# The sample group's states two at a time, in a hybrid decoder step on one core

## The chip, the cores and the metric

The kernel runs on one core of a Trainium2 chip. The metric is the device time of one execution in microseconds; of three runs of the kernel before the median is given. A core has TensorE (PE; matrix products and transposes), VectorE (DVE), ScalarE (ACT), GpSimd (POOL), and SyncE (SP), whose queue issues the DMAs here. Each works through its own instruction stream in order.

## The reference

One layer of a decoder serves a prompt (1024 tokens behind 16 learned ones) and a sample group of 8 sequences with one new token each. Two kinds of heads stand side by side: 8 delta-net heads, with a state S of 128 x 128 per head and sequence, and 4 matrix heads (mLSTM), with a state C of 128 x 256. For the sample group a step is, per sequence and head, with one token (L = 1), cut from the chunked form:

```python
u = _rms_norm(x, norm_w) @ w_in               # q, k, v, gates for both kinds of heads
# delta-net head, one token: kS = k @ S, qS = q @ S
v_new = beta * (v - exp(g) * kS)
o     = exp(g) * qS + (q . k) * v_new
S_new = exp(g) * S + outer(k, v_new)
# matrix head, one token
num   = dec * (q @ C) + ws * (q . k) * v
C_new = dec * C + outer(ws * k, v)
y = concat(gated, normed heads) @ w_out ; x + y, then a last RMSNorm
```

All states go out again as outputs; each is read and written once. The states are 8 x 8 x 128 x 128 and 8 x 4 x 128 x 256 numbers of 4 bytes, 4 MB each.

## The kernel before

The projection by `w_in` is computed in float32 as three products of high and low parts (tiles `pjg`, `pjm`, `pjz`, `pjo`, `pjzm`: 128 x 128 weights against some 350 tokens). This stream of products is the filler: `filler` (L1891) yields four products at a time, and all else is written as generators ("threads") that a planner, `Plan` (L65 to L247), steps through while it records the program. The planner has a clock for each engine, reckons each instruction's time by its size (`note`, L99), and steps a thread when the planned time of what it yielded has come; if none is due, TensorE gets filler. So one fixed order per engine is written down. A thread that yields a tile is due when the tile is done by the plan, plus 2.5 us where a DMA made it (`DMA`, L72, and `when`, L178), or plus the thread's own margin, for the samples 1.5 us, and 1.0 more behind GpSimd (L179 to L180). A DMA is planned as 0.45 us of generation, 0.65 of delay, its bytes over 360 KB per us (220 for rows that are spread over all partitions), and 0.9 at the end for a load or 0.45 for a store (L108 to L113), behind the DMAs planned before it.

The sample group's states are worked on by one thread, `samples` (L1963): `gdn_sample` (L1130) for the delta-net heads, then `mlstm_sample` (L1377). A state of one head, or half a matrix head, is a tile of 128 x (8 x 128): eight sequences side by side, 512 KB. Two buffers, `db` and `ebuf[0]`, take turns (`sb`), and `ebuf[1]` (`vb`) holds the new values. For one state in turn, before the change:

- TensorE multiplies, for each of the 8 sequences, 32 columns (`knf` or `qf`) with that sequence's 128 columns of the state, in column tiles of 32: four products side by side fill 128 rows of one bank (L1190 to L1192, L1423 to L1425). In the trace float32 products have two passes each, so the 8 are 16.
- ScalarE copies the results, TensorE turns them (two transposes), and VectorE takes the wanted columns and makes the new values, 128 x 8.
- TensorE turns the new values to 8 x 128, ScalarE copies them, they go to DRAM (`vb_d`), and come back spread over all 128 partitions (`vb`).
- GpSimd multiplies `vb` by the key, VectorE multiplies the state by its decay (L1224, L1441), then adds `vb` (L1226, L1443), and the state is stored.

The next state is loaded into the other buffer in the meantime. For the matrix heads the new values are the projected ones, so `vb_d` is filled at the head's start.

Meanwhile the prompt's chains run: `mlstm_chain` (L1273) steps through nine chunks a head (tiles `mup`, `mnm`, `C`, `mpm`), and later `gate` (L1482) scales and turns the heads' outputs (`ht`, `hT`), with scales in `rsg` that `head_norms` (L1583) computes. When the samples are done, `places` (L1643) gives their buffers to the output weights.

Of the kernel before, what the change touches and what calls it, by code (L numbers as in the profile page):

```python
# [12 lines left out]
F32 = mybir.dt.float32  # L13
# [7 lines left out]
P = 128  # L21
# [4 lines left out]
NS = 8  # L26
# [270 lines left out]
def hymba_kernel(ctx: ExitStack, tc: tile.TileContext, a: dict, o: dict):  # L297
# [17 lines left out]
    def room(tag):  # L315
        return plan.room(tag, BANKS[tag])
# [133 lines left out]
    rsg = gp.tile([P, GH + MH, 8], F32, name="rsg")  # L450
# [32 lines left out]
    nrow = wk.tile([1, D], F32, tag="tmp", name="nrow", bufs=1)  # L483
# [645 lines left out]

    def gdn_sample():  # L1130
# [47 lines left out]
        rows = [e.rearrange("p a b -> p (a b)")[:, 384:512] for e in (wa, wb)]  # L1178
# [3 lines left out]
        sp.dma_start(sb[0], a["s_S"][0])  # L1182
        for h in range(GH):
            s_ = sb[h % 2]
            yield s_
            yield kn
            h0 = min(h, GH - 2)
            yield room("k")
            at = pst2(f"sA{h}")
            for b in range(NS):  # L1190
                g, j = divmod(b, 4)
                pe.matmul(at[32 * j : 32 * j + 32, P * g : P * g + P], knf[:, 16 * h0 : 16 * h0 + 32], s_[:, b, :], start=True, stop=True)  # L1192
            yield at
            for g in range(2):
                act.copy(rows[g], at[:, P * g : P * g + P])
            yield rows[1]
            for g in range(2):
                pe.transpose(at[:, 256 + P * g : 256 + P * g + P], rows[g], ident)
            yield at

            def of(i):
                c = 256 + 16 * (h - h0) + 8 * i
                return at[:, c : c + 33 * NS - 32 : 33]

            dve.tensor_tensor(out=sn[:, 3, h], in0=of(0), in1=eg[:, h], op=ALU.mult)
            dve.scalar_tensor_tensor(out=sn[:, 3, h], in0=vv[:, h], scalar=0.5, in1=sn[:, 3, h], op0=ALU.mult, op1=ALU.subtract)
            dve.tensor_tensor(out=sn[:, 3, h], in0=sn[:, 3, h], in1=bet[:, h], op=ALU.mult)
            dve.tensor_tensor(out=sn[:, 4, h], in0=of(1), in1=eg[:, h], op=ALU.mult)
            dve.tensor_tensor(out=sn[:, 5, h], in0=sn[:, 3, h], in1=r[:, 5, h], op=ALU.mult)
            dve.tensor_tensor(out=sn[:, 4, h], in0=sn[:, 4, h], in1=sn[:, 5, h], op=ALU.add)  # L1210
# [4 lines left out]
            vsb = wk.tile([NS, P], F32, tag="vsb", name=f"vsb{h}")  # L1215
            act.copy(vsb, vp[0:NS, 0:P])
            sp.dma_start(vb_d[8 * h : 8 * h + 8], vsb)
# [159 lines left out]
    def mlstm_sample():  # L1377
# [27 lines left out]
        rows = wa.rearrange("p a b -> p (a b)")[:, 256:512]  # L1405
# [3 lines left out]
        sp.dma_start(sb[0], a["s_C"][0, 0])  # L1409
        for h in range(MH):  # L1410
            for i in range(2):
                yield room("k")
                vp = pst2(f"mvt{h}_{i}")
                pe.transpose(vp[0:NS, 0:P], msam[:, 2 + i, h], ident)
                vsb = wk.tile([NS, P], F32, tag="vsb", name=f"mvsb{h}_{i}")
                act.copy(vsb, vp[0:NS, 0:P])
                sp.dma_start(vb_d[h, i], vsb)
            for i in range(2):
                s_ = sb[i]
                yield s_  # L1420
                yield room("k")
                qt = pst2(f"mqc{h}_{i}")
                for b in range(NS):  # L1423
                    g, j = divmod(b, 4)
                    pe.matmul(qt[32 * j : 32 * j + 32, P * g : P * g + P], qf, s_[:, b, :], start=True, stop=True)  # L1425
                vb = ebuf[1]
                sp.dma_start(vb, vb_d[h, i].partition_broadcast(P))
                if (h, i) != (MH - 1, 1):
                    sp.dma_start(sb[1 - i], a["s_C"][h + i, 1 - i])
                yield qt  # L1430
                act.copy(rows, qt[:, 0:256])
                yield rows
                for g in range(2):
                    pe.transpose(qt[:, 256 + P * g : 256 + P * g + P], rows[:, P * g : P * g + P], ident)
                qc = qt[:, 256 + 8 * h : 256 + 8 * h + 33 * NS - 32 : 33]
# [46 lines left out]
    def gate(kt_, wcol):  # L1482
# [15 lines left out]
        for c in range(8):  # L1498
            act.activation(ht[:, c], ht[:, c], AF.Copy, scale=rsg[:, hh, c : c + 1])
# [556 lines left out]
```

## Time and profile before

| | |
|---|---|
| runs, us | 1205.81, 1203.74, 1205.92; median 1205.81 |
| profiled execution, us | 1202.72 |
| its span, first to last instruction, us | 1200.9 |
| TensorE products busy | 1184.0 us, 99% |
| VectorE busy | 852.2 us, 71% |
| ScalarE busy | 602.4 us, 50% |
| GpSimd busy | 487.9 us, 41% |
| first and last product of the delta-net states, us | 643.6, 809.4 |
| first and last product of the matrix states, us | 867.4, 968.2 |

Busy times of engines overlap. TensorE's products are pipelined, and an entry's length is that of one pass from its start to its modelled end; what a product costs the stream is read from one start to the next. An idle time stands in brackets behind the instruction that it precedes, with what ended it.

### The profile page before, as it was taken

The numbers are of one execution on the slowest core, as the hardware profiler recorded it, in microseconds if no ns is written. First come the engines' busy times: TensorE is split into PE (matmuls) and PEld (weight loads), VectorE is DVE, ScalarE is ACT, GpSimd is POOL, SyncE is SP. The second block draws the span as 40 slices with busy tenths as digits, with TensorE's granted clock in tenths as the row PEclk, the third lists the DMA queues.
The fourth block names the chain that finished last, engine by engine and source line by source line (L and its number), as shares of the span: only waits on it lengthen the run. The fifth ranks groups of instructions, "written<-read, shape, count | busy, mean of one in ns | idle before, by whom it ended". The sixth has DMA issues, their size and how long they took to land.

```text
span 1200.9 us, 23024 instructions
## 1 busy us (share of the span) xinstructions
PE 1184.0 (99%) x8314; PEld 1105.9 (92%) x8314; DVE 852.2 (71%) x2069; ACT 602.4 (50%) x1894; POOL 487.9 (41%) x648
## 2 busy tenths in 40 slices
PE   9999999999999999999999999999999999999997
PEld 7999999999999999999999999999999999876885
DVE  6789787587968588864356665546767665887986
ACT  7544455667565666554544453336543433333544
POOL 3105977827685756864012404230011111441432
PEclk9999999999999999999999999999999999999999
DMA  6032212212221221122122443535778878574352
GB/s 242 19 97 86 81 47 83 87 43 72 69 75 43 89 73 55 36 75 61 43 84 70 154 126 119 174 123 172 273 273 286 305 269 297 204 270 132 107 159 87
DMA packets 87084, 154.86 MB, mean 129 GB/s; under 512 B 26793, under 2 KB 48513, under 8 KB 86970
## 3 DMA queue, kind: packets, MB, share of 16 engines
q1 hardware_dynamic: 86776, 153.23, 38.1%
q8 instruction: 65, 1.06, 0.4%
q14 instruction: 49, 0.40, 0.1%
q10 hardware_dynamic: 194, 0.17, 0.0%
HBM read 107.65 MB, written 45.71 MB: 128 GB/s over the span
## 4 chain that ended last, share of the span: by engine, by line
PE 82%; DVE 9%; issue 5%; ACT 1%; POOL 1%; DMA 1%; POOLq 0%; SPq 0%; DVEq 0%; ACTq 0%
PE pjg L56 20%; PE pjm L56 13%; PE pjo L56 7%; PE pjz L56 7%; PE op L56 7%; PE pjzm L56 7%; PE up L56 4%; PE tp L56 3%; PE sk L56 2%; PE mnm L56 2%; DVE left L56 1%; PE mup L56 1%; PE hT L56 1%; DVE owl L56 1%; PE kk L56 1%
## 5 line engine op out<-in xcount | busy, mean ns | idle before, releaser
L56 PE MATMUL pjg<-xht,whg 128*128 128x350 f32 (+6 forms) x624 | 197.6, 324 | 1.0 <-ACT xht L56 1.0
L56 PE MATMUL pjg<-xlt,whg 128*128 128x350 f32 (+6 forms) x624 | 197.1, 323 | 0.0
L56 PE MATMUL pjg<-xht,wlg 128*128 128x350 f32 (+6 forms) x592 | 191.1, 326 | 0.0
L56 POOL TENSOR_TENSOR tmp<-B,E 33x31 f32<-33x31 f32 (+15 forms) x248 | 147.0, 593 | 75.3 <-DMA B<-nd 56.5
L56 POOL TENSOR_TENSOR E<-E,tmp 33x31 f32<-33x31 f32 (+15 forms) x248 | 156.0, 629 | 19.4
L56 PE MATMUL op<-owh,left 128*128 128x512 f32 x448 | 142.0, 396 | 2.1 <-DVE xr L56 1.8
L56 PE MATMUL pjm<-xht,wlm 128*128 128x350 f32 (+2 forms) x384 | 126.4, 329 | 0.0
L56 PE MATMUL pjm<-xht,whm 128*128 128x350 f32 (+2 forms) x384 | 126.4, 329 | 0.0
L56 PE MATMUL pjm<-xlt,whm 128*128 128x350 f32 (+2 forms) x384 | 126.2, 329 | 0.0
L56 PEld LDWEIGHTS pjg<-xht,whg 128*128 128x128 f32 x624 | 116.5, 189 | 1.8 <-issue 1.2
L56 PEld LDWEIGHTS pjg<-xlt,whg 128*128 128x128 f32 x624 | 116.5, 189 | 0.5
L56 PEld LDWEIGHTS pjg<-xht,wlg 128*128 128x128 f32 x592 | 111.0, 189 | 0.4
L56 PEld LDWEIGHTS op<-owh,left 128*128 128x128 f32 x448 | 84.0, 188 | 24.7 <-DVE xr L56 2.6
L56 DVE SCALAR_TENSOR_TENSOR kq<-cr,prm,kq 128x346 f32<-128x346 f32 (+7 forms) x147 | 92.1, 630 | 11.6 <-ACT cr L56 8.3
L56 PE MATMUL op<-owl,left 128*128 128x512 f32 x224 | 88.3, 394 | 0.0
L56 PEld LDWEIGHTS pjm<-xht,wlm 128*128 128x128 f32 x384 | 72.5, 189 | 0.8 <-issue 0.4
L56 PEld LDWEIGHTS pjm<-xlt,whm 128*128 128x128 f32 x384 | 72.4, 188 | 0.6 <-issue 0.4
L56 PEld LDWEIGHTS pjm<-xht,whm 128*128 128x128 f32 x384 | 72.4, 189 | 0.2
L56 POOL TENSOR_TENSOR ebuf<-ebuf,wb 128x1024 f32<-128x1024 f32 x8 | 15.7, 1965 | 122.7 <-DMA ebuf<-mvb_d 122.7
L56 PE MATMUL pjo<-xht,who 128*128 128x344 f32 x192 | 62.3, 324 | 0.6 <-DVE mg L56 0.6
L56 PE MATMUL pjz<-xlt,whz 128*128 128x344 f32 x192 | 62.8, 327 | 0.0
L56 PE MATMUL pjz<-xht,wlz 128*128 128x344 f32 x192 | 62.4, 325 | 0.0
(353 smaller groups left out, 3180.7 us busy)
## 6 DMA issues: line engine op xcount, KB each, us to landing
wrg<-in_wt SPq DMA_DIRECT2D x23, 512.0 KB
left<-c_d SPq DMA_DIRECT2D x40, 256.0 KB
wrm<-in_wt SPq DMA_DIRECT2D x16, 512.0 KB
ht<-h_d SPq DMA_DIRECT2D x16, 512.0 KB
gm<-rows_d SPq DMA_DIRECT2D x8, 576.0 KB
xt<-in_x_p SPq DMA_DIRECT2D x8, 512.0 KB
wrz<-in_wt SPq DMA_DIRECT2D x8, 512.0 KB
h_d<-oo SPq DMA_DIRECT2D x64, 64.0 KB
```

The costliest lines, as they stand in the source:

```text
L56: r = f(*args, **kw)
```

## The change

The states are taken in pairs. Both buffers are loaded, and one group of 16 products in column tiles covers both (one bank of 512 columns). Four columns' worth of rows are copied to a new tile `srow` and turned by four transposes into a second bank. In the delta-net heads the new values of two heads are turned by one transpose (16 x 128) and stored by one DMA; each head's are then spread in turn into the one `vb`. GpSimd no longer multiplies `vb`: it multiplies the state by its decay. VectorE does the rest in eight instructions a state, one a sequence, each `vb` times the key's column plus the decayed state. The next pair is loaded when both states have been read for their stores by the plan.

Beside this, the scales `rsg` become one tile for the delta-net heads and one for each matrix head, `gate` yields that tile, and the first row `nrow` lives under another tag.

```diff
-    rsg = gp.tile([P, GH + MH, 8], F32, name="rsg")
+    rsg = [(gp.tile([P, 1, 8], F32, name=f"rsm{h}"), 0) for h in range(MH)]
+    rsg += [(gp.tile([P, GH, 8], F32, name="rsg"), h) for h in range(1)]
+    rsg += [(rsg[MH][0], h) for h in range(1, GH)]
...
-    nrow = wk.tile([1, D], F32, tag="tmp", name="nrow", bufs=1)
+    nrow = wk.tile([1, D], F32, tag="E", name="nrow", bufs=1)
...
+    srow = gp.tile([P, 4 * P], F32, name="srow")
...
-        sp.dma_start(sb[0], a["s_S"][0])
-        for h in range(GH):
-            s_ = sb[h % 2]
-            yield s_
-            yield kn
-            h0 = min(h, GH - 2)
+        for i in range(2):
+            sp.dma_start(sb[i], a["s_S"][i])
+        for h in range(0, GH, 2):
+            for x in (*sb, kn):
+                yield x
             yield room("k")
             at = pst2(f"sA{h}")
-            for b in range(NS):
-                g, j = divmod(b, 4)
-                pe.matmul(at[32 * j : 32 * j + 32, P * g : P * g + P], knf[:, 16 * h0 : 16 * h0 + 32], s_[:, b, :], start=True, stop=True)
+            for i in range(2):
+                for b in range(NS):
+                    g, j = divmod(b, 4)
+                    g = P * (g + 2 * i)
+                    pe.matmul(at[32 * j : 32 * j + 32, g : g + P], knf[:, 16 * h : 16 * h + 32], sb[i][:, b, :], start=True, stop=True)
             yield at
...
+            turned = pst2(f"sT{h}")
+            for g in range(4):
+                pe.transpose(turned[:, P * g : P * g + P], srow[:, P * g : P * g + P], ident)
...
-            pe.transpose(vp[0:NS, 0:P], sn[:, 3, h], ident)
+            pe.transpose(vp[0 : 2 * NS, 0:P], sn[:, 3, h : h + 2].rearrange("p h b -> p (h b)"), ident)
...
-            sp.dma_start(vb, vb_d[8 * h : 8 * h + 8].partition_broadcast(P))
-            if h + 1 < GH:
-                sp.dma_start(sb[(h + 1) % 2], a["s_S"][h + 1])
-            yield vb
-            pool.tensor_tensor(out=vb, in0=vb, in1=kn[:, h, 0].unsqueeze(2).to_broadcast([P, NS, P]), op=ALU.mult)
-            dve.tensor_tensor(out=s_, in0=s_, in1=eg[:, h].unsqueeze(2).to_broadcast([P, NS, P]), op=ALU.mult)
-            yield vb
-            dve.tensor_tensor(out=s_, in0=s_, in1=vb, op=ALU.add)
-            sp.dma_start(o["s_S"][h], s_)
+            for i in range(2):
+                hi, s_ = h + i, sb[i]
+                sp.dma_start(vb, vb_d[8 * hi : 8 * hi + 8].partition_broadcast(P))
+                pool.tensor_tensor(out=s_, in0=s_, in1=eg[:, hi].unsqueeze(2).to_broadcast([P, NS, P]), op=ALU.mult)
+                yield s_
+                yield vb
+                for b in range(NS):
+                    dve.scalar_tensor_tensor(out=s_[:, b], in0=vb[:, b], scalar=kn[:, hi, 0, b : b + 1], in1=s_[:, b], op0=ALU.mult, op1=ALU.add)
+                yield s_, 0.3
+                sp.dma_start(o["s_S"][hi], s_)
+            if h + 2 < GH:
+                yield plan.read[sb[0].tensor.name]
+                sp.dma_start(sb[0], a["s_S"][h + 2])
+            if h + 2 < GH:
+                yield plan.read[sb[1].tensor.name]
+                sp.dma_start(sb[1], a["s_S"][h + 3])
...
         yield has("rs", hh)
+        yield rsg[hh][0]
```

`mlstm_sample` is changed in the same way (two halves of a head are its pair; its new values are still turned one by one).

TensorE at the first delta-net pair (`sA`: the states' products; `pjm`: projection; `mup`, `mnm`: the prompt chain). Before, the first state's group and then, 112 rows later, the second one's:

```order
L56 MATMUL pjm1_2_2_8853<-xlt_77,whm1_2_8663 128x348
L56 MATMUL pjm1_2_2_8853<-xht_76,wlm1_2_8664 128x348
L56 MATMUL sA0_8881<-db_103,skn_8821 32x128 x8
L56 MATMUL mup0_1_8845<-va1_153,mkt0_1_8847 128x257
L56 MATMUL mnm0_1_8891<-C0_0_8839,mwq0_8607 128x257
```

```order
L56 MATMUL pjm1_3_2_9156<-xht_76,whm1_3_8779 128x348
L56 MATMUL pjm1_3_2_9156<-xlt_77,whm1_3_8779 128x348
L56 MATMUL sA1_9193<-ebuf0_101,skn_8821 32x128 x8
L56 MATMUL pjm1_3_2_9156<-xht_76,wlm1_3_8780 128x348
L56 MATMUL pjm1_3_2_9156<-xht_76,whm1_3_8779 128x348
```

After:

```order
L56 MATMUL pjm1_2_2_8859<-xlt_77,whm1_2_8668 128x348
L56 MATMUL pjm1_2_2_8859<-xht_76,wlm1_2_8669 128x348
L56 MATMUL sA0_8887<-db_103,skn_8826 32x128 x8
L56 MATMUL sA0_8887<-ebuf0_101,skn_8826 32x128 x8
L56 MATMUL mup0_1_8851<-va1_158,mkt0_1_8853 128x257
L56 MATMUL mnm0_1_8905<-C0_0_8845,mwq0_8612 128x257
```

The second group moved up to the first, with nothing between.

SyncE's queue from the first state's store to the loads of the next ones (`wrm`: weights; `mgm`: rows of the prompt's gates; `out_p_C`, `out_p_n`: the prompt's states). Before, with the second load of `db` behind its store by three DMAs:

```order
L56 DMA out_s_S<-db_103 128x1024
L56 DMA wrm2_2_9206<-in_wt 128x1024
L56 DMA vb_d_8826<-vsb1_9279 8x128
L56 DMA ebuf1_102<-vb_d_8826 128x1024
L56 DMA db_103<-in_s_S 128x1024
L56 DMA wrm2_3_9336<-in_wt 128x1024
L56 DMA out_s_S<-ebuf0_101 128x1024
```

After, from the store of the pair's first state; both loads of the next pair stand behind the second store:

```order
L56 DMA out_s_S<-db_103 128x1024
L56 DMA ebuf1_102<-vb_d_8831 128x1024
L56 DMA wrm2_2_9218<-in_wt 128x1024
L56 DMA out_p_C<-C0_8_9195 128x256
L56 DMA out_p_n<-C0_8_9195 128x1
L56 DMA mgm1_9226<-rows_d_84 128x1152
L56 DMA out_s_S<-ebuf0_101 128x1024
L56 DMA db_103<-in_s_S 128x1024
L56 DMA wrm2_3_9340<-in_wt 128x1024
L56 DMA ebuf0_101<-in_s_S 128x1024
```

The load of `db` moved from the middle of the next state's work to the end of the pair's, and that of `ebuf0` from behind `ebuf1`'s spread rows to just behind its own store.

VectorE at the first state's update (`mst`, `hst`: the prompt's norms; `mpm`, `C0`: the prompt chain; `wlm`: a weight's low part). Before:

```order
L56 SCALAR_TENSOR_TENSOR hst_106<-mst0_6_9107 128x1
L56 TENSOR_TENSOR mpm0_8_9140<-mup0_8_9135,mgm0_8606 128x128
L56 TENSOR_TENSOR db_103<-db_103,sgb_97 128x1024
L56 TENSOR_TENSOR wlm2_0_9077<-wrm2_0_8727,whm2_0_9076 128x256
L56 SCALAR_TENSOR_TENSOR C0_8_9166<-C0_7_9125,dec_94,mup0_8_9135 128x257
```

After:

```order
L56 SCALAR_TENSOR_TENSOR hst_106<-mst0_6_9130 128x1
L56 TENSOR_TENSOR mpm0_8_9163<-mup0_8_9158,mgm0_8611 128x128
L56 SCALAR_TENSOR_TENSOR db_103<-ebuf1_102,skn_8826,db_103 128x128 x8
L56 TENSOR_TENSOR wlm2_0_9100<-wrm2_0_8732,whm2_0_9099 128x256
L56 SCALAR_TENSOR_TENSOR C0_8_9195<-C0_7_9148,dec_94,mup0_8_9158 128x257
```

The decay's product has left VectorE, and the eight scaled additions, which read the spread rows in `ebuf1`, stand in its place ahead of the chain's `C0_8`; the addition of before stood 11 rows further down.

## Rows read from the trace of the kernel before

**Rows 1.** the page's part 1: busy us, share of the span, instructions.

```profile
PE 1184.0 (99%) x8314; PEld 1105.9 (92%) x8314; DVE 852.2 (71%) x2069; ACT 602.4 (50%) x1894; POOL 487.9 (41%) x648
```

**Rows 2.** a stretch: us, busy us by engine, granted clock, DMA share, GB/s.

```profile
640.00:985.00 345.00, 342.03 (x2354) 324.44 (x2354) 218.23 (x560) 154.72 (x480) 67.23 (x49) 1.00 0.58 200
```

**Rows 3.** timeline, TensorE: start us, us, instruction, count, [idle before <-releaser].

```profile
668.27 0.32 PE L56 MATMUL pjm<-xht,whm 128*128 128x348 f32 x1
668.43 0.32 PE L56 MATMUL pjm<-xlt,whm 128*128 128x348 f32 x1
668.68 0.64 PE L56 MATMUL sA<-ebuf,skn 128*32 128x128 f32 x16
669.26 0.42 PE L56 MATMUL pjm<-xht,wlm 128*128 128x348 f32 x1
669.52 0.32 PE L56 MATMUL pjm<-xht,whm 128*128 128x348 f32 x1
```

**Rows 4.** timeline, TensorE, one head's two transposes.

```profile
671.93 0.27 PE L56 MATMUL sA<-ident,wa 128*128 128x128 f32 x1
672.04 0.27 PE L56 MATMUL sA<-ident,wb 128*128 128x128 f32 x1
```

**Rows 5.** tile sA: ns min/median/max, first and last start, forms.

```profile
L56 PE MATMUL sA<-db,skn x64: 272/273/298, 643.6 to 788.8; 128*32 128x128 f32 x64
```

**Rows 6.** timeline, TensorE, one head's new values turned.

```profile
676.39 0.32 PE L56 MATMUL pjm<-xht,whm 128*128 128x344 f32 x1
676.55 0.27 PE L56 MATMUL svt<-ident,wa 128*8 128x128 f32 x1
...
676.82 0.32 PE L56 MATMUL pjm<-xht,wlm 128*128 128x344 f32 x1
```

**Rows 7.** groups, VectorE: form, count, busy us, mean ns, idle before.

```profile
L56 DVE TENSOR_TENSOR ebuf<-ebuf,ebuf 128x1024 f32<-128x1024 f32 x8 | 12.7, 1584 | 0.0
...
L56 DVE TENSOR_TENSOR ebuf<-ebuf,sgb 128x1024 f32<-128x1024 f32 x8 | 12.1, 1509 | 0.0
...
L56 DVE TENSOR_TENSOR db<-db,ebuf 128x1024 f32<-128x1024 f32 x8 | 9.8, 1220 | 2.9 <-POOL ebuf L56 2.8
```

**Rows 8.** timeline, VectorE, four scaled products of 128 columns.

```profile
450.55 1.12 DVE L56 SCALAR_TENSOR_TENSOR N<-kk,kap,gm 128x128 f32<-128x128 f32 x4
```

**Rows 9.** timeline, DMA queue and GpSimd: rows spread, and used.

```profile
705.14 0.33 SPq L56 DMA_DIRECT2D ebuf<-vb_d  x1
...
709.60 1.90 POOL L56 TENSOR_TENSOR ebuf<-ebuf,skn 128x1024 f32<-128x1024 f32 x1 [18.23 <-DMA ebuf<-vb_d]
...
966.32 0.55 SPq L56 DMA_DIRECT2D ebuf<-mvb_d  x1
...
974.85 1.90 POOL L56 TENSOR_TENSOR ebuf<-ebuf,wb 128x1024 f32<-128x1024 f32 x1 [10.25 <-DMA ebuf<-mvb_d]
```

**Rows 10.** timeline, DMA queue: a store, and the load held for it.

```profile
937.98 0.34 SPq L56 DMA_DIRECT2D out_s_C<-db  x1
...
944.18 0.33 SPq L56 DMA_DIRECT2D db<-in_s_C  x1
...
983.40 0.34 SPq L56 DMA_DIRECT2D out_s_C<-ebuf  x1
988.01 0.81 SPq L56 DMA_DIRECT2D ebuf<-in_wo  x2
```

**Rows 11.** timeline, TensorE: the products of the state loaded at 944.18.

```profile
953.42 0.64 PE L56 MATMUL mqc<-db,msam 128*32 128x128 f32 x16
```

**Rows 12.** timeline, TensorE: its longest idle times from 640 to 985 us.

```profile
644.56 0.46 PE L56 MATMUL mup<-va,mkt 128*128 128x257 f32 x1 [0.34 <-DVE mpm L56]
...
817.25 0.55 PE L56 MATMUL hT<-ident,ht 128*128 128x128 f32 x3 [1.16 <-ACT va L56]
...
845.05 0.32 PE L56 MATMUL sosum<-wa,ones 128*128 128x64 f32 x1 [0.50 <-DVE wa L56]
...
846.08 0.43 PE L56 MATMUL pjo<-xht,who 128*128 128x344 f32 x1 [0.59 <-DVE mg L56]
```

More of the change, by code (lines that the diff above doesn't have):

```diff
@@ new lines, in gdn_sample, with of @@
+            for g in range(4):
+                pe.transpose(turned[:, P * g : P * g + P], srow[:, P * g : P * g + P], ident)
+            yield turned
+            for i in range(2):
+                hi = h + i
+                def of(k):
+                    c = 272 * i + 8 * k
+                    return turned[:, c : c + 33 * NS - 32 : 33]
+                dve.tensor_tensor(out=sn[:, 3, hi], in0=of(0), in1=eg[:, hi], op=ALU.mult)
+                dve.scalar_tensor_tensor(out=sn[:, 3, hi], in0=vv[:, hi], scalar=0.5, in1=sn[:, 3, hi], op0=ALU.mult, op1=ALU.subtract)
+                dve.tensor_tensor(out=sn[:, 3, hi], in0=sn[:, 3, hi], in1=bet[:, hi], op=ALU.mult)
+                dve.tensor_tensor(out=sn[:, 4, hi], in0=of(1), in1=eg[:, hi], op=ALU.mult)
+                dve.tensor_tensor(out=sn[:, 5, hi], in0=sn[:, 3, hi], in1=r[:, 5, hi], op=ALU.mult)
+                dve.tensor_tensor(out=sn[:, 4, hi], in0=sn[:, 4, hi], in1=sn[:, 5, hi], op=ALU.add)
@@ L1408, in mlstm_sample @@
         sb = (db, ebuf[0])
-        sp.dma_start(sb[0], a["s_C"][0, 0])
+        for i in range(2):
+            sp.dma_start(sb[i], a["s_C"][0, i])
         for h in range(MH):
+            yield room("k")
+            vp = pst2(f"mvt{h}")
+            vsb = wk.tile([2 * NS, P], F32, tag="vsb", name=f"mvsb{h}")
             for i in range(2):
[L1412 to L1417, printed above, removed]
+                pe.transpose(vp[0:NS, P * i : P * i + P], msam[:, 2 + i, h], ident)
+            act.copy(vsb[0:NS], vp[0:NS, 0:P])
+            sp.dma_start(vb_d[h, 0], vsb[0:NS])
+            vsb = wk.tile([2 * NS, P], F32, tag="vsb", name=f"mvsc{h}")
+            act.copy(vsb[0:NS], vp[0:NS, P : 2 * P])
+            sp.dma_start(vb_d[h, 1], vsb[0:NS])
+            for x in sb:
+                yield x
+            yield room("k")
+            qt = pst2(f"mqc{h}")
+            for i in range(2):
+                for b in range(NS):
+                    g, j = divmod(b, 4)
+                    g = P * (g + 2 * i)
+                    pe.matmul(qt[32 * j : 32 * j + 32, g : g + P], qf, sb[i][:, b, :], start=True, stop=True)
+            vb = ebuf[1]
+            sp.dma_start(vb, vb_d[h, 0].partition_broadcast(P))
+            yield qt
+            for i in range(2):
+                act.copy(srow[:, 256 * i : 256 * i + 256], qt[:, 256 * i : 256 * i + 256])
+            yield srow
+            yield room("k")
+            turned = pst2(f"mqT{h}")
+            for g in range(4):
+                pe.transpose(turned[:, P * g : P * g + P], srow[:, P * g : P * g + P], ident)
+            yield turned
@@ L1418, in mlstm_sample @@
             for i in range(2):
                 s_ = sb[i]
[L1420 to L1435, printed above, removed]
-                yield vb
-                pool.tensor_tensor(out=vb, in0=vb, in1=kw[:, h].unsqueeze(2).to_broadcast([P, NS, P]), op=ALU.mult)
+                qc = turned[:, 256 * i + 8 * h : 256 * i + 8 * h + 33 * NS - 32 : 33]
@@ L1440, in mlstm_sample @@
                 dve.tensor_tensor(out=num[:, i, h], in0=num[:, i, h], in1=t[:, 7, h], op=ALU.add)
-                dve.tensor_tensor(out=s_, in0=s_, in1=decb[:, h].unsqueeze(2).to_broadcast([P, NS, P]), op=ALU.mult)
+                pool.tensor_tensor(out=s_, in0=s_, in1=decb[:, h].unsqueeze(2).to_broadcast([P, NS, P]), op=ALU.mult)
+                yield s_
                 yield vb
-                dve.tensor_tensor(out=s_, in0=s_, in1=vb, op=ALU.add)
+                for b in range(NS):
+                    dve.scalar_tensor_tensor(out=s_[:, b], in0=vb[:, b], scalar=kw[:, h, b : b + 1], in1=s_[:, b], op0=ALU.mult, op1=ALU.add)
+                yield s_, 0.3
+                if i == 0:
+                    sp.dma_start(vb, vb_d[h, 1].partition_broadcast(P))
                 sp.dma_start(o["s_C"][h, i], s_)
+            for i in range(2 if h + 1 < MH else 0):
+                yield plan.read[sb[i].tensor.name]
+                sp.dma_start(sb[i], a["s_C"][h + 1, i])
         dve.tensor_tensor(out=t[:, 10:12], in0=num, in1=num, op=ALU.mult)
@@ L1589, in head_norms @@
             yield hst
[L1590 removed]
+            rsqrt_wide(rsg[h0][0], hst[:, n], rst[:, 0 : len(heads)])
             for i in range(len(heads)):
```

30 lines of the change are left out of this document (8 added, 22 removed).

## The prediction

> **What bounds the kernel now.** I read the page's busy times first. TensorE works 1184.0 of 1200.9 us, VectorE 71% and GpSimd 41% [rows 1]: TensorE is the bound, and work taken off another engine is worth only what it saves TensorE in waiting. Then the sums by stretch. The samples' products run from 640 to 985 us, and there TensorE is busy 342.03 of 345.00 us at a granted clock of 1.00, VectorE 218, GpSimd 67 [rows 2]. So the change acts where TensorE has some 3 us of idle time, and pays by TensorE instructions removed; waits added there are paid in full. Last I looked, at one group of products after another, at what TensorE pays for it, and who ended its idle times.
>
> **TensorE: the groups.** A plain projection product starts 0.16 us after the one before (668.27, 668.43 [rows 3]). From the last projection product ahead of a group of eight products (16 passes) to the second one behind it, 668.43 to 669.52, are 1.09 us; without the group it would be two steps, 0.32. So a group costs 0.77. Four 32-column passes run side by side over 128 columns; two full-width passes over 128 columns stand 0.11 apart (671.93, 672.04 [rows 4]), so the 16 passes are four such rounds, 0.44, and 0.33 is fixed: the step from full-width to column tiles and back. Before there are 16 such groups: 64 passes on db in the delta-net heads [rows 5] are four groups, ebuf has four more, and by the code the matrix heads as many. After there are eight groups of 32 passes: 0.33 + 8 x 0.11 = 1.21 each against 2 x 0.77 = 1.54. **Saved: 8 x 0.33 = 2.6 us.** Bounds: no group of 16 stands in the trace; if all of the fixed part recurred for the second eight, 0; more than the whole 0.33 cannot go. I take the 0.33, since the 16 products follow each other with nothing between (the order shows it).
>
> **TensorE: the turned values.** The turn of one head's new values costs 676.82 - 676.39 - 0.32 = 0.11 [rows 6], whatever its few columns. Eight become four in the delta-net heads: **4 x 0.11 = 0.4 us.** The four-at-a-time transposes of the copied rows are as many as before (0.11 each), the matrix heads' value turns too: nothing. Together 3.0 us off TensorE's 1184.
>
> **VectorE and GpSimd.** Before, a state costs VectorE a multiplication and an addition of 1024 elements: 9.8 us for eight on db, 12.1 and 12.7 on ebuf [rows 7]; the missing row of db is like its neighbour, so 44 us in all. After, a state costs eight scaled additions of 128 elements. Four such in a row (reading PSUM instead of a state) take 1.12 us with the first one's latency [rows 8], so about 0.26 a step, eight in 2.2 us, sixteen states in 35. VectorE gains some 9 us, hidden under TensorE's products. GpSimd keeps 16 instructions of the same shape, now decays; they no longer wait for the new values from DRAM, as the GpSimd rows did [rows 9], and nothing on TensorE waited for that: nothing. ScalarE copies two rows of 256 columns a pair instead of four of 128: nothing. The separate tiles for the norms' scales and the other home of the first row change only which waits are written: nothing, bounded by ScalarE's rows not appearing at the ends of TensorE's long waits but in one (below).
>
> **What the change adds: waits.** (a) The scaled additions stand on VectorE and need the new values spread from DRAM; before, GpSimd had that wait and VectorE only waited for GpSimd. Behind them on VectorE stands the next step of the chain (C0_8 in the order), for which TensorE's next chain product waits. The spread rows land 4.5 us after issue in the delta-net heads (705.14 to 709.60) and up to 8.5 in the matrix heads (966.32 to 974.85) [rows 9]; the plan puts the additions at least 2.5 us behind its own 4.4. So nothing in the delta-net heads, where the chain runs; at most 8.5 - 6.9 = 1.6 us a state later on, where nothing so tight is queued behind. I take 0.
>
> (b) Both buffers are now read by one group and both refilled after it. A state's load must wait until the old state is stored, at six places (three in each kind of head), and the next products wait for the later of two loads. From a store's issue to the load that the queue held back for it are 4.6 us (983.40 to 988.01) and 6.2 (937.98 to 944.18) [rows 10]; before, such a held-back load of the matrix heads was still early for its products (944.18 to 953.42 [rows 11]), because the other buffer's group lay between. A load takes what a spread takes, 4.5 to 8.5. So 9.1 us from store to products in a quiet stage and 14.7 in the worst. The plan reckons the store at 0.45 + 0.65 + 1.46 + 0.45 = 3.0, the load at 3.5, and waits 2.5 more: 9.0, and longer only where its own account of the queue is longer. Late by 0.1 us at the quiet places, by up to 5.7 at each of the three busy ones; the least is 0. DMA is busy 0.58 over the stretch [rows 2], so I take the quiet figure for most and **0.5 us in all**; both ends, 0 and 17, stay for the range. Behind the held load on SyncE stand weight loads and row stores, needed much later.
>
> The Trainium skill (DMA: Bandwidth & Descriptors, "Anatomy of one DMA") puts a DMA at about 2.0 us plus bytes over 436 GB/s, most of the fixed part being the receipt of the write, slowest to HBM. By it a store of 512 KB would be done in an estimated 3.2 us and the term (b) would be 0, the sum 3.0; the trace has 4.6 for it, and the measured figure stands.
>
> (c) TensorE's idle times now: 0.34 for the chain's VectorE product, 1.16 behind ScalarE, 0.50 and 0.59 behind VectorE at 845 and 846 [rows 12]. The last two fall beside the last delta-net update (VectorE busy with its addition); this sum product moves earlier by 94 other products in TensorE's order, so they can go, or come back somewhere else. Bounds -1.1 and +1.1; I take 0.
>
> **Sum.** 2.6 + 0.4 - 0.5 = 2.5 us off. The profiled execution took 1202.72 us (span 1200.9, 1.8 around it), 3.1 under the median of 1205.81 of the three runs shown; a fixed number of TensorE steps comes off either, so 1200.2 against it and **1203.3 us** against the median. A difference of less than 0.2%, 2.4 us, cannot be told from none: the forecast lies right at that edge.
>
> **Rivals.** *Less waiting as well.* The idle times behind VectorE (0.34, 0.50, 0.59) mostly go, since its updates shrink and no load comes late: 3.0 + 1.4 = 4.4 off, 1201.4. For it: VectorE's 9 us less and the moved sum product; against: those waits were accidents of neighbours, and new neighbours make new ones.
>
> *VectorE held up by GpSimd.* Half the states' VectorE work before took 1.51 and 1.58 us instead of 1.22 [rows 7]: those on ebuf, which meet GpSimd's work. If GpSimd's decays, which now run as soon as the products are done, meet VectorE's chain work in the same way, the waits behind VectorE (1.43) double: 3.0 - 0.5 - 1.4 = 1.1 off, 1204.7, no measurable change. The skill (GPSIMD Engine Reference, "Specifications") says that GpSimd's SBUF interfaces are shared with VectorE and contend with VectorE instructions of two SBUF inputs, as the scaled additions are. Against: the decays stand early, while the additions still wait for their rows.
>
> *Slower: the states come late.* The place is (b). With the busy figure (6.2 + 4.5 = 10.7, 1.7 late) at all three matrix-head places and half of that at the delta-net ones: 5.1 + 2.6 - 3.0 = 4.7 slower, 1210.5. It decides from 0.5 us late a place, which eats the 3.0. For it: two loads and two stores of 512 KB and a weight load follow each other on one queue. Against: the plan counts those bytes, and its margin is 2.5 us.
>
> **Chances.** Forecast 0.54, own range 1201.8 to 1205.0; less waiting 0.18; GpSimd 0.14; late states 0.14. Faster by over 0.2%: 0.18 + 0.33 of the forecast's, 0.51. Within: 0.20 + 0.13 and 0.02 of the late ones, 0.35. Slower: 0.14 in all, 0.12 of it late states, the rest the forecast's and GpSimd's tail. The range, 1200.0 to 1207.5, holds the first three cases with the runs' own spread of 1203.74 to 1205.92 and the lesser half of the late ones.
>
> **What will show it.** Right: groups of 32 passes between projection products cost about 1.2 us, TensorE's count of column-tile groups is eight, the scaled additions stand 0.26 apart, and the six places show no idle time on TensorE ahead of a group. Wrong: a group of 32 near 1.5; TensorE's rows for sA or mqc with an idle time ended by a state's load; chain products of the delta-net stage waiting longer for VectorE than 0.34; or the output products after 1026 us starting later than by TensorE's own saving.

## The result and the profile after

The changed kernel takes 1195.84 us (median of 6 runs, 1195.00 to 1197.06), the kernel before, run beside it, 1204.38 (1202.53 to 1205.92): a ratio of 0.9933 [0.9922, 0.9943], **some 8 us faster**. The forecast was 1203.3 us, in a range of 1200.0 to 1207.5; the time lies below the range. The profiled execution took 1197.06 us, span 1195.3.

TensorE's busy time fell from 1184.0 [rows 1] to 1181.2 us, in the page's first part:

```profile
PE 1181.2 (99%) x8310; PEld 1106.9 (93%) x8310; DVE 847.6 (71%) x2165; ACT 600.9 (50%) x1882; POOL 482.1 (40%) x648
```

The stretch of the samples' products, against [rows 2] (us, then busy us of PE, PEld, DVE, ACT, POOL, granted clock, DMA share, GB/s):

```profile
640.00:985.00 345.00, 344.32 (x2390) 330.38 (x2389) 216.72 (x674) 155.73 (x477) 64.88 (x50) 1.00 0.60 206
```

TensorE is busy 2.3 us more of the same 345 and gets more work done in it: 2390 records against 2354. Of its idle times before, [rows 12] showed the four longest, 2.59 us in sum. After the change two are left above 0.1 us, 0.60 in sum:

```profile
816.34 0.66 PE L56 MATMUL hT<-ident,ht 128*128 128x128 f32 x4 [0.39 <-ACT va L56]
...
843.12 0.43 PE L56 MATMUL pjo<-xht,who 128*128 128x344 f32 x1 [0.21 <-DVE mg L56]
```

A group of 32 passes, against [rows 3]:

```profile
690.47 0.32 PE L56 MATMUL pjm<-xlt,whm 128*128 128x350 f32 x1
690.72 0.65 PE L56 MATMUL sA<-db,skn 128*32 128x128 f32 x16
691.18 0.62 PE L56 MATMUL sA<-ebuf,skn 128*32 128x128 f32 x16
691.73 0.43 PE L56 MATMUL pjm<-xht,wlm 128*128 128x350 f32 x1
692.00 0.32 PE L56 MATMUL pjm<-xht,whm 128*128 128x350 f32 x1
```

692.00 - 690.47 - 0.32 = 1.21 us; the other groups that stand between projection products cost 1.20 or 1.21. On VectorE one state's eight scaled additions, against [rows 7, 8], in the timeline and then as a group of four states (count, busy us, mean ns; three more groups have the same 8.7):

```profile
667.07 2.18 DVE L56 SCALAR_TENSOR_TENSOR db<-ebuf,skn,db 128x128 f32<-128x128 f32 x8
```

```profile
L56 DVE SCALAR_TENSOR_TENSOR db<-ebuf,skn,db 128x128 f32<-128x128 f32 x32 | 8.7, 344 | 0.0
```

And two pairs' stores and held-back loads on the DMA queue, against [rows 10], with the products that read the second one:

```profile
913.75 0.41 SPq L56 DMA_DIRECT2D out_s_C<-ebuf  x1
...
920.74 0.33 SPq L56 DMA_DIRECT2D ebuf<-in_s_C  x1
...
947.06 0.34 SPq L56 DMA_DIRECT2D out_s_C<-ebuf  x1
...
950.06 0.33 SPq L56 DMA_DIRECT2D ebuf<-in_s_C  x1
```

```profile
957.97 0.62 PE L56 MATMUL mqc<-ebuf,msam 128*32 128x128 f32 x16
```

At the second place the load goes out 3.0 us after the store, and 7.9 later its products start without an idle time; at the first it goes out 7.0 after, the longest. At the six places it is 3.0 to 7.0 us, and the group starts 9.5 to 14.0 us after the store, nowhere with an idle time.

**Where the time went.** I count the projection and output products, of which both traces have as many, and take off that this execution of after reached the 600th product 1.1 us later. From the 600th product to the 4,500th (115 to 990 us in the trace of before) the changed kernel gains 6.0 us, all of it after 600 us, and another 0.5 by the last output product. Of the 6.0, 3.0 are fewer TensorE steps and 2.4 are recorded idle times (2.59 and two small ones of 0.15 and 0.23 before, 0.60 now). The 0.6 that remains stands in no bracket. That makes 6.5, against 8.1 by the runs: the profiled execution of before lies 1.7 us under the median of its kernel, that of after 1.2 above. Of the 93 executions of the kernel before that were run beside the experiments, 12 have a mean granted clock of 0.997 or less and take 1205.6 us on average, the others 1203.2; none of the changed kernel's twelve has such a clock.

The idle times that went have different sources. The 0.34 us at 644 is filled: the second half of the group now stands ahead of the chain product `mup` that waited (e1 below, which parts the halves, has the 0.34 back). The 0.50 and 0.59 at 845 come from GpSimd holding VectorE (e15 below). The 1.16 at 817 stood behind ScalarE's chain copy `va`, and ahead of that ScalarE copied two rows for the samples. Before:

```profile
815.87 0.24 ACT L56 COPY wa<-sA 128x128 f32<-128x128 f32 x1
816.01 0.25 ACT L56 COPY wb<-sA 128x128 f32<-128x128 f32 x1
...
816.84 0.35 ACT L56 COPY va<-mtp 128x256 f32<-128x256 f32 x1
```

After:

```profile
815.93 0.35 ACT L56 COPY va<-mtp 128x256 f32<-128x256 f32 x1
```

In the changed order no copies for the samples stand there, and four turns go ahead of the wait, of which 0.39 us is left; how much each of the two counts no run shows. This hangs on the order and not on the pairs as such: e9 below, in pairs too, has 0.80 us there.

### The profile page after: what moved, and what is told of

Same layout as the page of the kernel before. It is cut to its first block, busy times and chain, and to the rows that moved or that the text cites. A ratio compares the mean times of both kernels' runs of the same rounds, so it can differ in the third digit from the quotient of the medians.

```text
span 1195.3 us, 23095 instructions
## 1 busy us (share of the span) xinstructions
PE 1181.2 (99%) x8310; PEld 1106.9 (93%) x8310; DVE 847.6 (71%) x2165; ACT 600.9 (50%) x1882; POOL 482.1 (40%) x648
## 4 chain that ended last, share of the span: by engine, by line
PE 88%; DVE 7%; ACT 1%; DMA 1%; issue 1%; SPq 0%; POOLq 0%; POOL 0%; DVEq 0%; ACTq 0%
PE pjg L56 20%; PE pjm L56 15%; PE op L56 9%; PE pjz L56 8%; PE pjzm L56 7%; PE pjo L56 7%; PE up L56 4%; PE tp L56 3%; PE sk L56 2%; PE mnm L56 2%; PE mup L56 2%; PE mtp L56 1%; PE hT L56 1%; DVE left L56 1%; PE kk L56 1%
## 5 line engine op out<-in xcount | busy, mean ns | idle before, releaser
L56 POOL TENSOR_TENSOR mwq<-mt,mgm 128x384 f32<-128x384 f32 x12 | 10.8, 897 | 168.2 <-DVE mgm L56 168.2
L56 POOL TENSOR_TENSOR db<-db,sgb 128x1024 f32<-128x1024 f32 x8 | 16.4, 2051 | 151.8 <-PE mqc L56 113.7
```

Of the source, the lines that this page charges most:

```text
L56: r = f(*args, **kw)
```

## The experiments

The theories by their letters: A, VectorE's new updates take TensorE's waits away; B, the pairs do, by re-ordering the samples' steps (E: since there are half as many steps); C, the split scales do; D, any new order moves the waits by several us, and this was a good draw; later F, GpSimd holds VectorE and VectorE holds TensorE, against G, the engines' own queues.

"Gain" below is the gain on the kernel before by that same count, from the 600th to the 4,500th product of the one profiled execution. That execution is one of those timed; in e10 and e13 it is the slowest of them, so there the gain lies under what the runs show. In e6 and e7 42 TensorE records of the samples' work still stand behind the 4,500th product, in e1, e12, e16 and e17 four, which flatters the gain there: by the end of the projection it is 0.5 in e12, and 0.5 lower in e1, e16 and e17. Times are medians; the difference comes from the ratio of the runs.

| run | us | ratio [95%] | against before, us | gain, us |
|---|---|---|---|---|
| changed kernel | 1195.84 | 0.9933 [0.9922, 0.9943] | -8.1 | 6.0 |
| e1, groups split | 1199.43 | 0.9966 [0.9955, 0.9976] | -4.1 | 2.8 |
| e2, updates only | 1201.79 | 0.9998 [0.9984, 1.0012] | -0.2 | 0.1 |
| e3, scales only | 1204.19 | 1.0010 [0.9998, 1.0021] | +1.2 | -3.4 |
| e4, before, margin 1.2 | 1201.21 | 0.9983 [0.9972, 0.9994] | -2.0 | 0.4 |
| e5, changed again | 1195.31 | 0.9929 [0.9914, 0.9945] | -8.5 | 6.8 |
| e6, pairs only | 1212.83 | 1.0074 [1.0058, 1.0090] | +8.9 | 6.8 |
| e7, pairs, scales | 1213.22 | 1.0083 [1.0064, 1.0102] | +10.0 | 5.9 |
| e8, pairs, updates | 1196.69 | 0.9939 [0.9922, 0.9957] | -7.3 | 5.4 |
| e9, changed, margin 1.2 | 1204.00 | 1.0005 [0.9995, 1.0015] | +0.6 | -1.2 |
| e10, before, gate 1.5 | 1201.18 | 0.9979 [0.9970, 0.9989] | -2.5 | -1.0 |
| e11, changed, gate 1.5 | 1196.65 | 0.9933 [0.9920, 0.9946] | -8.1 | 4.9 |
| e12, before, margin 1.9 | 1201.07 | 0.9979 [0.9970, 0.9988] | -2.5 | 2.5 |
| e13, e9, short decays | 1199.98 | 0.9967 [0.9954, 0.9979] | -4.0 | -0.8 |
| e14, changed, short decays | 1197.67 | 0.9942 [0.9929, 0.9956] | -7.0 | 4.8 |
| e15, before, short products | 1201.59 | 0.9981 [0.9971, 0.9991] | -2.3 | 0.6 |
| e16, ScalarE's decays | 1196.92 | 0.9943 [0.9930, 0.9955] | -6.9 | 5.8 |
| e17, changed, margin 1.9 | 1198.77 | 0.9954 [0.9940, 0.9967] | -5.5 | 4.2 |
| e18, changed, gate 2.5 | 1199.45 | 0.9959 [0.9946, 0.9971] | -4.9 | 2.3 |

**e1: the group of 16 as two of 8.**

```diff
             for i in range(2):
+                if i:
+                    yield plan.clock["pe"] + 0.01
                 for b in range(NS):
```

> The changed kernel with projection products put between the two halves of each group of 16 (8 sequences, then others, then 8). If what a group costs TensorE is a fixed 0.33 us and 0.11 a round of four passes, the fixed part comes back eight times: 2.6 us above the changed kernel's 1195.8, about 1198.5, 6 us below the kernel before, and each half costs 0.77. If the whole gain of 8.5 us came from taking the products in one run, it returns to 1203 to 1205. If the step from full width to column tiles costs nothing in fact and only waits went, it stays at 1195.8.

TensorE's timeline of a half:

```profile
865.52 0.31 PE L56 MATMUL pjzm<-xht,whzm 128*128 128x344 f32 x1
865.76 0.64 PE L56 MATMUL mqc<-db,msam 128*32 128x128 f32 x16
866.34 0.42 PE L56 MATMUL pjzm<-xlt,whzm 128*128 128x344 f32 x1
866.60 0.32 PE L56 MATMUL pjzm<-xht,wlzm 128*128 128x344 f32 x1
```

866.60 - 865.52 - 0.32 = 0.76 a half, 1.53 a pair: the 2.6 us of the groups are confirmed. The run is 4.0 above the changed kernel. Of the other 1.4, 0.34 is the wait that the undivided group had filled; the rest lies within what a new order does (below):

```profile
644.28 0.67 PE L56 MATMUL mup<-va,mkt 128*128 128x257 f32 x2 [0.34 <-DVE mpm L56]
```

**e2 and e3: the updates alone, the scales alone, on the kernel before.** e2 exchanges the updates as in the change, one state at a time, in both kinds of heads; e3 takes the `rsg` tiles and the gate's wait for them.

```diff
 e2
-            pool.tensor_tensor(out=vb, in0=vb, in1=kn[:, h, 0]..., op=ALU.mult)
-            dve.tensor_tensor(out=s_, in0=s_, in1=eg[:, h]..., op=ALU.mult)
-            dve.tensor_tensor(out=s_, in0=s_, in1=vb, op=ALU.add)
+            pool.tensor_tensor(out=s_, in0=s_, in1=eg[:, h]..., op=ALU.mult)
+            for b in range(NS):
+                dve.scalar_tensor_tensor(out=s_[:, b], in0=vb[:, b], scalar=kn[:, h, 0, b : b + 1], in1=s_[:, b], ...)
 e3
+        yield rsg[hh][0]
```

> The kernel before, one state at a time, with only the updates exchanged: GpSimd multiplies the state by its decay, VectorE does eight scaled additions of 128 columns. Theory A (VectorE's shorter updates take away the idle times of TensorE): the 5.5 us that the instruction count leaves unexplained come here, 1198 to 1200. Theory B (those waits went because the pairs re-ordered the sample's steps): no change, 1203.5 to 1205.5. Theory C (the scales' tile): no change here either.

> The kernel before with only the norm scales split into a tile for the delta-net heads and one for each matrix head, and the gate waiting for that tile. Theory C (the split takes away ScalarE's wait at 817 us, 1.16 to 0.39, and finer ones of the gates): 0.8 to 3 us faster, 1201.5 to 1203.6. Theories A and B: within 0.8 us of 1204.4.

Neither part alone gains beyond its interval: C falls, and A falls for single states. (e2's median is 1.2 us below that of the kernel before; three of its twelve executions, at 1205.7 to 1207.3 us, bring the ratio to 1.) e3's trace shows what a late order costs (timeline of TensorE, and stretches):

```profile
872.05 0.32 PE L56 MATMUL pjzm<-xlt,whzm 128*128 128x344 f32 x1
873.03 2.38 PE L56 MATMUL hT<-ident,ht 128*128 128x128 f32 x8 [0.67 <-ACT ht L56]
...
876.12 0.49 PE L56 MATMUL pjo<-xht,who 128*128 128x344 f32 x1
876.41 0.49 PE L56 MATMUL pjo<-xlt,who 128*128 128x344 f32 x1
```

```profile
870.00:875.00 5.00, 4.33 (x23) 3.03 (x21) 0.87 (x2) 2.42 (x8) 0.00 (x0) 1.00 1.02 392
875.00:880.00 5.00, 5.00 (x23) 4.90 (x23) 3.90 (x5) 1.29 (x4) 2.13 (x1) 0.66 0.87 343
```

The turns wait 0.67 us for ScalarE and then go at its pace, 2.1 us for eight, which is no bracketed idle time. Behind that the granted clock falls to a mean of 0.66 (part of the stretch at 1.2 in place of 2.4 GHz), and products stand 0.29 apart instead of 0.16. The idle time of 0.67, the slow turns and the lower clock together cost 3.4 us.

**e5 to e8: the changed kernel again, and its pairs with less of the rest.** e6 keeps the pairs alone, e7 the pairs and the scales, e8 the pairs and the updates. e6 and e7 have, in the pairs' loops (the matrix heads' alike):

```diff
-                pool.tensor_tensor(out=s_, in0=s_, in1=eg[:, hi]..., op=ALU.mult)
-                yield s_
                 yield vb
-                for b in range(NS):
-                    dve.scalar_tensor_tensor(out=s_[:, b], in0=vb[:, b], scalar=kn[:, hi, 0, b : b + 1], in1=s_[:, b], ...)
+                pool.tensor_tensor(out=vb, in0=vb, in1=kn[:, hi, 0]..., op=ALU.mult)
+                dve.tensor_tensor(out=s_, in0=s_, in1=eg[:, hi]..., op=ALU.mult)
+                yield vb
+                dve.tensor_tensor(out=s_, in0=s_, in1=vb, op=ALU.add)
```

> The changed kernel once more, unchanged, beside its parts below. If its saving is of TensorE's instructions and of idle times that its order has for good, it is again 7 to 9 us below the kernel before, with no execution in which TensorE's clock falls in mid-kernel. If part of it was chance of the few executions, 3 to 6 us.

> Only the pairs: groups of 16, turns of two heads, both loads behind the group; GpSimd multiplies the new values by the key and VectorE multiplies and adds over 1024 elements as before, the scales are one tile. Instructions alone: 3.0 us below the kernel before, 1200. Theory E (half as many steps of the samples means half as many places where the samples' copies on ScalarE and work on VectorE stand ahead of what TensorE waits for): 5.5 to 8.5 us below, 1194.5 to 1197.5. Theory D (the order drawn by the change): anything from 1 to 5 below, and nowhere near 1195.8.

> The changed kernel with the updates of the kernel before (GpSimd multiplies the new values, VectorE multiplies and adds over 1024 elements). Theory A (VectorE's updates): the extra 5.5 us are lost, about 1200. Theory E (pairs): 1194.5 to 1197.5. Theory D: 1 to 5 below the kernel before.

> The changed kernel with the norm scales in one tile as before. Theory C (scales): 1 to 3 us above the changed kernel. Theory E: within 1 us of it, 1195 to 1197. Theory D: 2 us or more away from it either way, since the steps of the planner shift.

No theory had e6 and e7 slower than before. Up to the 4,500th product they gain about as much as the changed kernel, in part because work of the samples is still to come; then e6 loses 19 us (TensorE's timeline, the DMA queue, one stretch):

```profile
1025.45 1.03 PE L56 MATMUL mms<-wb,ones 128*128 128x32 f32 x4 [3.45 <-DVE wb L56]
1036.10 0.79 PE L56 MATMUL op<-owh,left 128*128 128x512 f32 x1 [9.62 <-ACT owh L56]
```

```profile
1023.88 0.34 SPq L56 DMA_DIRECT2D out_s_C<-ebuf  x1
...
1026.59 1.70 SPq L56 DMA_DIRECT2D ebuf<-in_wo  x2
```

```profile
1028.00:1032.00 4.00, 0.00 (x0) 0.00 (x0) 3.52 (x14) 0.00 (x0) 0.00 (x0) 0.50 1.01 382
```

The last state is stored at 1023.9, when the projection has run out; in the changed kernel at 980.2. Only then can the output weights (`in_wo`) be loaded into the samples' buffers. The delta-net groups start 67, 60.5 and 59 us apart in e6 (643.5, 710.8, 771.3, 830.5) and 46 to 49 in the changed kernel. Between the groups of two pairs both states' updates stand one after the other on the one `vb`. In e6 GpSimd's product stands behind the spread rows and the plan's margins behind that: from the issue of the spread rows to the state's store a delta-net state takes 11.2 to 23.8 us, in the changed kernel 7.6 to 14.2. With single states the next state's group lay between, which would cover this time; that e2 shows nothing agrees, but no run isolates it.

e8 is 1.4 us above e5, just beyond the 1 us that E allowed and inside the 1 to 3 us of C. Its order differs from the changed kernel's as well, so this doesn't show what the scales are worth.

**e4, e9, e12, e17: the samples' margin; e10, e11, e18: the gates'.** The work is the same in each, the order is another. e12 and e17 have 1.9 for 1.2, e18 has 2.5 for 1.5; e10 and e12 start from the kernel before, as e4 does.

```diff
-SAMPLE = 1.5
+SAMPLE = 1.2
...
-        yield ht
+        yield ht, 1.5
         if kt_ < 8:
```

> The kernel before with the samples thread's planned margin at 1.2 us in place of 1.5: the same work, other places in the order. Theory D (any new order moves TensorE's waits by several us, and the change drew a good one): the time moves by 2 us or more either way. Theories A to C: within 1 us of 1204.4.

> The changed kernel with the samples' planned margin at 1.2 us in place of 1.5: the same work, other places in the order. Theory E (pairs take waits away wherever they stand, since there are half as many of the samples' steps): within 1.2 us of the changed kernel, 1194.3 to 1196.7, and the projection and output products from 600 to 990 us gain 5 to 7 us on the kernel before. Theory D (this order was a lucky one): 1197.5 to 1201, with idle times back at other places.

> The kernel before with the gates' turns (hT) planned 1.5 us behind ScalarE's scaling in place of 0.45. If TensorE's waits at those turns (1.16 us at 817, and slower turns after) are worth what they show, 1.2 to 1.8 us below the kernel before. If a wait that is moved away comes back at the next place, within 0.7 us of it.

> The changed kernel with the same larger margin of the gates' turns. Its turns wait for ScalarE 0.6 us in all, so 0 to 0.6 us below the changed kernel, 1194.8 to 1195.6; a new order's waits, if theory D holds, put it up to 2 us away on either side.

> The kernel before with the samples' planned margin at 1.9 us. Theory E: within 2 us of the kernel before, since there are as many steps of the samples as before; the gain from 600 to 990 us lies between -1 and +3.5, as in the other kernels with one state at a time. Theory D: it may reach as far as 4 us below, where the pairs begin.

> The changed kernel with the samples' planned margin at 1.9 us in place of 1.5. If an order of the pairs is as a rule 3 us (TensorE's instructions) below an order of the single states, whose own lie from 1201 to 1204, this one lies from 1198 to 1201. If the pairs are good for the waits in most orders, 1195 to 1197.5.

> The changed kernel with the gates' turns planned 2.5 us behind ScalarE's scaling in place of 0.45. As for the run with 1.5 us: 1194.5 to 1197 if the pairs are good in most orders; 1198 to 1201 if the instructions alone are the rule.

e9 fells theory E: 0.3 us of a planned margin takes the whole gain of the pairs, more than D's 1197.5 to 1201 allowed too. With single states e4, e10 and e12 are each 2.0 to 2.5 us below the kernel before: more than the 1 us that A to C left for e4 and the 1.8 that the turns' waits promised for e10. e11 stays at the changed kernel. e17 and e18 come out between 1198 and 1201, where the instructions alone were put, and not where pairs that are good in most orders would be. e9's trace at 844 us (GpSimd; VectorE; TensorE; stretches):

```profile
844.71 1.91 POOL L56 TENSOR_TENSOR db<-db,sgb 128x1024 f32<-128x1024 f32 x1 [52.33 <-DVE rst L56]
846.58 2.44 POOL L56 TENSOR_TENSOR ebuf<-ebuf,sgb 128x1024 f32<-128x1024 f32 x1
```

```profile
844.07 0.17 DVE L56 TENSOR_TENSOR rsm<-rsm,rst 128x8 f32<-128x8 f32 x1
...
844.88 1.76 DVE L56 TENSOR_TENSOR rsm<-rsm,rst 128x8 f32<-128x8 f32 x1
...
847.17 0.50 DVE L56 SCALAR_TENSOR_TENSOR mg<-thzm,pjzm 128x344 f32<-128x344 f32 x1
847.70 1.69 DVE L56 SCALAR_TENSOR_TENSOR mg<-to,mg 128x344 f32<-128x344 f32 x1
```

```profile
845.55 0.32 PE L56 MATMUL pjzm<-xht,wlzm 128*128 128x344 f32 x1
847.73 0.43 PE L56 MATMUL pjo<-xht,who 128*128 128x344 f32 x1 [1.85 <-DVE mg L56]
```

```profile
844.00:848.00 4.00, 2.15 (x39) 1.67 (x39) 3.79 (x9) 1.00 (x3) 3.29 (x2) 1.00 0.97 336
848.00:852.00 4.00, 4.00 (x21) 3.94 (x21) 3.42 (x5) 1.26 (x5) 1.02 (x1) 0.61 0.88 267
```

The same instruction on 8 columns takes 0.17 us and, when it meets GpSimd's decay, 1.76: it ends when GpSimd ends (844.71 + 1.91 = 846.62). So the `mg` at 847.17 is late, the product that waits for it idles 1.85 us, and the clock falls. The next `mg`, at 847.70, meets the second decay and takes 1.69 us. The kernel before has the like at 836 us (GpSimd; VectorE):

```profile
836.43 1.90 POOL L56 TENSOR_TENSOR ebuf<-ebuf,skn 128x1024 f32<-128x1024 f32 x1 [33.20 <-DMA ebuf<-vb_d]
```

```profile
836.45 1.90 DVE L56 TENSOR_TENSOR rst<-rst,hst 128x8 f32<-128x8 f32 x1
838.39 0.17 DVE L56 TENSOR_SCALAR rst<-rst 128x8 f32<-128x8 f32 x1
```

The Trainium skill (Trainium Architecture — The Big Picture, "What this means for kernel authors") calls the ports that VectorE and GpSimd share an exclusive lock, not a split of bandwidth; both traces agree: what is 0.17 us alone takes 1.76 and 1.90 and ends with GpSimd's instruction.

e11 shows how near the loads run: `ebuf`'s half of a group waits for its state at two places, here and 0.25 at 961.08.

```profile
736.79 0.64 PE L56 MATMUL sA<-ebuf,skn 128*32 128x128 f32 x16 [0.18 <-DMA ebuf<-in_s_S]
```

**e13 to e15: every engine's order kept, GpSimd's instruction on the states cut to one column in 128.** The other columns are left out. The plan still counts the long instruction, so no instruction moves (e13 starts from e9; e15 does the same to `vb`, whose product with the key it leaves out but for that column):

```diff
-                pool.tensor_tensor(out=s_, in0=s_, in1=eg[:, hi]..., op=ALU.mult)
+                pool._eng.tensor_tensor(out=s_[:, :, 0:1], in0=s_[:, :, 0:1], in1=eg[:, hi].unsqueeze(2), op=ALU.mult)
+                plan.note("pool", "tensor_tensor", s_, [s_, eg[:, hi]...], None, False)
```

> The changed kernel with margin 1.2 (1204.0), every engine's order the same, but GpSimd decays only one column in 128 of each sequence's state (the other 127 are left out), so that its 16 instructions are short. Theory F (GpSimd holds VectorE for the length of its instruction, VectorE is late for TensorE, and TensorE's clock falls behind a long wait): the waits of 1.85 at 848 and 0.87 at 957 and the lower clock behind the first (1.7) go, 1198.5 to 1200.5. Rival G (VectorE's and ScalarE's own queues at that order): 1203 to 1204.5.

> The changed kernel with the same shortening, every engine's order the same. Theory F: its decays hold VectorE at no place for which TensorE then waits long, so 0 to 0.6 us below 1195.5. Rival G: the same 1195 to 1196.

> The kernel before, every engine's order the same, with GpSimd's multiplication of the new values done on one column in 128 of each sequence (the others are left out). Theory F: the wait at 836 of VectorE's norms (1.90 for 8 columns) goes, with it TensorE's 0.50 and 0.59 at 845, and in some executions the lower clock behind them: 1 to 2.5 us below the kernel before. Rival G: within 0.5 us; ScalarE's 1.16 at 817 stays in both.

e13, the places of e9's rows (VectorE; TensorE, the second row with a later wait; ScalarE):

```profile
843.68 0.17 DVE L56 TENSOR_TENSOR rsm<-rsm,rst 128x8 f32<-128x8 f32 x1
...
844.36 0.51 DVE L56 SCALAR_TENSOR_TENSOR mg<-thzm,pjzm 128x344 f32<-128x344 f32 x1
844.90 0.52 DVE L56 SCALAR_TENSOR_TENSOR mg<-to,mg 128x344 f32<-128x344 f32 x1
```

```profile
844.93 0.43 PE L56 MATMUL pjo<-xht,who 128*128 128x344 f32 x1 [0.25 <-DVE mg L56]
...
891.70 1.65 PE L56 MATMUL hT<-ident,ht 128*128 128x128 f32 x5 [2.60 <-ACT ht L56]
```

```profile
891.25 0.98 ACT L56 ACTIVATE ht<-ht,rsg 128x128 f32<-128x128 f32 x3 [4.78 <-DMA ht<-h_d]
```

The held instructions are back at 0.17 and 0.52, 1.85 of idle time became 0.25, 0.87 at 957 is gone, and the run is 4 to 5 us faster than e9: theory F holds for these waits. A new one came, 2.60 us at 891.70, for rows that landed late from DRAM, with a fall of the clock behind it; so the count up to 990 us hardly moved in this profiled execution. In e15 the two waits of 0.50 and 0.59 are gone likewise:

```profile
844.97 0.33 PE L56 MATMUL sosum<-wa,ones 128*128 128x64 f32 x2
845.10 0.40 PE L56 MATMUL pjo<-xht,who 128*128 128x344 f32 x1
```

and it is 2.3 us [1.1, 3.5] faster, within F's 1 to 2.5. Its profiled execution gains only 0.6 by the count; where the rest lies no trace shows. e14 is some 1 us above the changed kernel, within the intervals, and not below, which neither F nor G had: in its profiled execution the gates' rows land late from DRAM, and the turns at 846 go at ScalarE's pace, 2.1 us for eight.

**e16: the decays on ScalarE**, in place of GpSimd's instruction:

```diff
+                for b in range(NS):
+                    act.activation(s_[:, b], s_[:, b], AF.Copy, scale=eg[:, hi, b : b + 1])
+                    if b % 2:
+                        yield plan.clock["act"] + 0.4
```

> The changed kernel with the decays on ScalarE, eight scalings of 128 columns a state, two at a time, in place of GpSimd's one instruction (a new order for all engines). Theory F: no wait behind a held VectorE from 640 to 985 us, but some 34 us more on ScalarE, for whose scalings TensorE's turns wait: 1194.5 to 1199. Rival G: as any other order of the pairs, 1195 to 1204.

No wait behind a held VectorE, and three behind ScalarE (0.41, 0.58, 0.41). The time lies in the ranges of both F and G, so it doesn't part them. No kernel beats the changed one beyond its interval.

## Why the prediction was wrong

Of the 7.5 us between forecast and result 1.4 are the base: the three runs that the forecast starts from have a median of 1205.81, the six beside the changed kernel 1204.38. The other 6 are saving that the sum didn't have (2.5 us forecast, 8.1 by the ratio).

- *TensorE's groups and turned values, 3.0 us*: right. 1.21 a group (rows above), eight groups, e1 at 0.76 a half. The 0.4 of the turned values was not tested by itself; the trace has four such turns where that of before has eight.
- *(c), waits of TensorE, taken as 0 with bounds of 1.1 either way*: **the step that failed.** The bounds took only the two waits of 0.50 and 0.59 [rows 12] as open to change, and only as idle times. In this order 2.4 us of idle time went, 1.16 to 0.39 behind ScalarE among them, and 0.6 that stands in no bracket; other orders bring back as much and more (e9). With the 3.0 above and 0.5 at the output products that is the 6.5 of the traces; the other 1.6 of the runs' 8.1 no trace shows. The rival "less waiting as well" had the direction, at 1.4. In e3 a held-up step cost five times its bracket (3.4 us for 0.67), since turns went at ScalarE's pace and the clock fell behind it; and the [rows 2] clock of 1.00 is one execution's.
- *(b), state loads late, 0.5 us*: not paid in this order; 0.43 in e11. The loads themselves were as late as the sum's busy figure, up to 7.0 us behind the store against 6.2. But the groups started 9.5 to 14.0 us behind the store, where the sum had taken the plan's shortest, 9.0, for all six. The Trainium skill (DMA: Bandwidth & Descriptors, "Anatomy of one DMA") gives the 2.0 us, which the prediction quotes, for DMAs issued by GpSimd; here SyncE issues them, and the queue's own 3.0 to 7.0 us decide. A loss of the size of the upper bound, 17, came by another way: with the old updates the samples end 44 us later and the output weights come late (e6).
- *VectorE and GpSimd, worth nothing*: true for single states (e2, -0.2 us), wrong for pairs. e6 and e8 differ by the updates alone: 16 us. Under the pairs the time from the spread rows to the store, GpSimd's place and the plan's margins included, sets the pace of the pairs and the end of the samples.
- *Rival "VectorE held up by GpSimd"*: its mechanism is what the waits at 845 us are made of (e9, e13, e15). In the changed kernel's order the decays hold VectorE too, but where nothing on TensorE is soon due; no idle time of TensorE follows this one, 1.6 us longer than the like of it elsewhere:

```profile
893.73 2.15 DVE L56 SCALAR_TENSOR_TENSOR mg<-to,mg 128x344 f32<-128x344 f32 x1
```

- *The scales' tiles, worth nothing*: not told from the order's own spread (e3, and e8 against the changed kernel).

How much of the 8 us is the change's? Six kernels with single states and all of the work (before, e2, e3, e4, e10, e12) lie from -2.5 to +1.2 against before, mean -1.0. Six with pairs and the new updates (changed, e8, e9, e11, e17, e18) lie from -8.3 to +0.6, mean -5.6. The means differ by 4.6, with a standard error of about 1.5 from these spreads: 3.0 of instructions and a remainder that this doesn't tell from nothing. By this reckoning the rest of the 8 is a good place among the planner's orders. Whether pairs are also better for the waits on the whole stays open: six orders each, all near the first one, are few.

## What to carry to other kernels

Where an order is written out by a planner, time a change in several orders (two or three margins moved a little) before crediting its mechanism: here the orders of one and the same work spread over 2.5 us with single states and 9 with pairs, where the change itself is worth 3.0. Look for tiny instructions with a long duration beside a GpSimd instruction; they mark the places where a shift of a microsecond decides. An edit that is worth nothing by itself can carry the other one (the pairs alone lose 9 us, the updates alone gain nothing, both together gain 7 to 8): after each part, ask which chain now sets the pace and what waits for its end.

## What was not expected of the hardware

- A VectorE instruction with two SBUF inputs and 8 columns took 1.76 (e9) and 1.90 us (before) beside GpSimd's 1024-column one, and 0.17 with that one shortened and the order kept (e13, e15).
- Behind an idle time of 0.67 us and turns at a slow pace (e3), and behind 1.85 (e9), TensorE's granted clock fell to means of 0.66 and 0.61 over the next 5 and 4 us, though products followed without an idle time; behind 1.16 [rows 12] it did not. The fall came behind 2.10 us in e10 (0.57 over 4 us) and 2.60 in e13 as well, and not behind 0.94 in e18.
